# Two long passes, two short ones, and a later norm in the up stage of a transformer block

## The chip, the cores and the metric

The kernel runs on one core of one Trainium2 chip. Its time is device microseconds of one execution. Five engines work side by side, each on a queue of its own in fixed order: TensorE (PE; its loads of the stationary operand are shown apart as PEld), VectorE (DVE), ScalarE (ACT), GpSimd (POOL) and SyncE (SP), which here only issues DMA transfers. They wait for each other by semaphores. TensorE reads SBUF and writes PSUM, which has eight banks of 128 x 512 fp32 numbers.

## The reference, cut to what matters

One block of a model with 256 tokens and width 2048, all in fp32. After three kinds of attention and a gate comes the part that the change touches:

```python
h2 = rms_norm(x, g_ffn)
u = causal_depthwise_conv(h2 @ w_up, conv_w, conv_b)   # w_up: 2048 x 11264, 3 taps along the sequence
u_gate, u_val = split(u, 2)                            # 5632 columns each
x = x + (silu(u_gate) * u_val) @ w_down
```

The causal convolution works on each column of h2 @ w_up by itself: y[t] = w0 u[t-2] + w1 u[t-1] + w2 u[t] + b, with zeros before the first token.

## The kernel before, in words

A fp32 number is split in two parts: hi, rounded to the format that TensorE multiplies at full rate, and lo, what is left. A product of two fp32 matrices is then three products of parts (hi hi, lo hi, hi lo). For a weight tile that is: a DMA to a raw tile (the SP queue), a cast to hi on ScalarE (L141) and a subtraction that gives lo on VectorE (L142), all in `piece`. Raw, hi and lo tiles have four buffers each, so a piece's hi and lo are written when the piece four before it has been read.

**The up stage** (L1133 to L1154) computes the columns of h2 @ w_up transposed, with 128 columns on the partitions and the 256 tokens along the free dimension. It works in 22 *rounds*: for each block of 512 columns (f0) one round for the gate half (s = 0) and one for the value half (s = 1). A round fills four PSUM banks, one for each 128 columns, over 16 k tiles of 128 rows, loaded two at a time: eight pieces, named by their first k tile (k=0, 2, ... 14). The moving operand hT holds hi and lo of the hidden state side by side, 256 columns each. For each k tile and bank there are two passes:

- a *long* pass (L1148): the weight's hi part against all 512 columns of hT. The bank's left half gets hi hi, its right half hi lo.
- a *short* pass (L1149): the weight's lo part against the first 256 columns, added to the left half.

That makes 64 *pairs* a round, 1408 in the stage. They follow each other long, short, long, short.

**The row norm** of h2 isn't applied to hT; it is a factor for each token and may be multiplied in after the product. Its sums are taken from the new x while round one runs. Then L1044 writes the 256 factors to DRAM and L1045 reads them back to all partitions, both on GpSimd's queue, into the tile rbc, 128 x 256.

**The convolution** of one bank is `conv` (L1109 to L1129): a copy of the bank's right half (ScalarE, L1114), the left half added (VectorE, L1116), the product with rbc into a padded tile u (L1117), the three taps (ScalarE L1120, VectorE L1121 and L1122), and for the gate half Silu (L1124), for the value half the product with the gate (L1128) and a split in hi and lo for the next stage (L175, L176). There are two tiles u, used in turn, six tiles y, and two tiles cr for the sum of the halves.

**The order of work.** `later` puts a generator in a list; `tick`, called once a piece (a *step*), lets the two oldest run up to their next `yield`, which may name a number of steps to sit out. So the four convolutions of a round run in the first two steps of the next round, two a step. Beside them two background generators (`weight_sums`, L243 to L274) prepare sums of tiles of w_down for the next stage: loads pre_d on SP, three additions on VectorE (L267 to L269), a store. Within that, a scheduler settles each engine's order, except for instructions given to `in_order`, which stay in the order of the program.

Of the kernel before, what the change touches and what calls it, by code (L numbers as in the profile page):

```python
# [9 lines left out]
F32 = mybir.dt.float32  # L10
F32R = mybir.dt.float32r
AF = mybir.ActivationFunctionType
ALU = mybir.AluOpType
AX = mybir.AxisListType

P = 128
S = 256
# [24 lines left out]
def hybrid_block(  # L42
# [25 lines left out]
    nc = tc.nc  # L68
# [12 lines left out]
    def bank(name):  # L81
        return pp.tile([P, 512], F32, tag="bank", name=name)
# [14 lines left out]
    def later(gen):  # L97
        waiting.append(gen)
# [3 lines left out]
    def tick(beside=True):  # L102
        if beside:
            for g in background:
                next(g, None)
        while waiting and len(active) < WINDOW:
            active.append([waiting.popleft(), 0])
        for a in list(active):
            if a[1] > 0:
                a[1] -= 1  # L110
                continue
            try:
                a[1] = next(a[0]) or 0
            except StopIteration:
                active.remove(a)
# [19 lines left out]
    def piece(src, a, n, name):  # L135
        raw = wp.tile([P, PIECE], F32, tag="raw", name=f"raw_{name}")
        hi = wp.tile([P, PIECE], F32R, tag="hi", bufs=SBUFS, name=f"hi_{name}")
        lo = wp.tile([P, PIECE], F32R, tag="lo", bufs=SBUFS, name=f"lo_{name}")
        m = a * n
        pin(nc.sync.dma_start(raw[:, :m].rearrange("p (a n) -> p a n", a=a), src))  # L140
        pin(nc.scalar.copy(hi[:, :m], raw[:, :m]))  # L141
        pin(nc.vector.tensor_tensor(lo[:, :m], raw[:, :m], hi[:, :m].bitcast(F32), ALU.subtract))  # L142
        return (
            hi[:, :m].rearrange("p (a n) -> p a n", a=a),
            lo[:, :m].rearrange("p (a n) -> p a n", a=a),
        )
# [9 lines left out]
    def product(x_of, w, nk, n0, n, name):  # L156

        ps = [bank(f"{name}_{t}") for t in range(NT)]
        wv = w.rearrange("(k p) n -> p k n", p=P)
        for k in range(0, nk, 2):  # L160
            a = min(2, nk - k)
            wh, wl = piece(wv[:, k : k + a, n0 : n0 + n], a, n, f"{name}_{k}")
            order = [(j, t) for j in range(a) for t in range(NT)]
            if k + a == nk:
                order.sort(key=lambda jt: jt[1])
            for j, t in order:
                xk = x_of(k + j)
                xs_ = xk[:, t * P : (t + 1) * P], xk[:, S + t * P : S + (t + 1) * P]
                three(ps[t][:, :n], *xs_, (wh[:, j], wl[:, j]), k + j == 0, k + j == nk - 1)
            tick()  # L170
        return ps

    def split_to(dst, src):

        nc.scalar.copy(dst[..., :S], src)  # L175
        nc.vector.tensor_tensor(dst[..., S:], src, dst[..., :S].bitcast(F32), ALU.subtract)  # L176
# [25 lines left out]
    def k_tiles(name):  # L202

        most = xt_pool.tile([P, KT - 2, 2 * S], F32R, tag="xt", name=name)
        rest = []

        def at(k):
            if k < KT - 2:
                return most[:, k]
            if not rest:  # L210
                rest.append(xt_pool.tile([P, 2, 2 * S], F32R, tag="xu", name=f"{name}_rest"))
            return rest[0][:, k - KT + 2]

        at.pair = lambda p: most[:, 2 * p : 2 * p + 2]
        return at
# [14 lines left out]
    in_order = tc.keep_in_program_order  # L230
# [343 lines left out]
    def plain_heads(ps, rs, name):  # L574
        y = rows_of(block(f"y_{name}"))
        for t in range(NT):
            nc.scalar.activation(y[:, t], ps[t], AF.Copy, scale=rs[:, t : t + 1])
        return y

    def norm_heads(ps, rs, name):  # L580

        y = plain_heads(ps, rs, name)
        ss = sm.tile([P, NT * 4], F32, tag="hss", name=f"hss_{name}")
        for t in range(NT):
            sq = junk(f"sq_{name}_{t}")
            nc.scalar.activation(sq, y[:, t], AF.Square)
            nc.vector.tensor_reduce(
                ss[:, t * 4 : (t + 1) * 4], sq.rearrange("p (h d) -> p h d", h=4), AX.X, ALU.add
            )
        r = sm.tile([P, NT * 4], F32, tag="hr", name=f"hr_{name}")  # L590
        rsqrt_mean(r, ss, NT * 4, HD, name)
        for t in range(NT):
            yt = y[:, t].rearrange("p (h d) -> p h d", h=4)
            nc.vector.tensor_tensor(
                yt, yt, r[:, t * 4 : (t + 1) * 4].unsqueeze(2).to_broadcast([P, 4, HD]), ALU.mult
            )
        return y
# [74 lines left out]
    for k in range(KT):  # L672
# [18 lines left out]
        for _ in range(0 if k < 3 else 1 if k < 8 else 3):  # L691
            if squares:
                j, t = squares.popleft()
# [9 lines left out]
    y = norm_heads(kv[0], rstd_m, "mk")  # L703
# [26 lines left out]
    ps = proj(C_MQ, MEM_W, "mq")  # L730
# [5 lines left out]
    y = norm_heads(ps, rstd, "mq")  # L736
# [30 lines left out]
    for c in range(3):  # L767
        ps = proj(c * 512, 512, f"f{c}")
        qk[c] = heads_of(block(f"qk_fox{c}"))
        y = norm_heads(ps, rstd, f"f{c}")  # L770
# [5 lines left out]
    ps = proj(1536, 512, "f3")  # L776
# [3 lines left out]
    ps = proj(2048, 262, "f4")  # L780
# [74 lines left out]
    for c in range(3):  # L855
        ps = proj(C_SB + c * 512, 512, f"s{c}")
        qs[c] = heads_of(block(f"qk_sb{c}"))
        y = plain_heads(ps, rstd, f"s{c}")
# [49 lines left out]
    ps = proj(C_SB + 1536, 512, "s3")  # L908
# [4 lines left out]
    ps = proj(C_SB + 2048, 256, "s4")  # L913
# [39 lines left out]
    for m in range(2):  # L953
        gate = []
        for b, plan in enumerate(g_plans[m]):
# [40 lines left out]
            if not plan:  # L996
                biases()
                for n in range(2):
                    ps = proj(c0 + n * 512, 512, f"g{n}_{b}")
# [12 lines left out]
        for n in range(2):  # L1012
            acc = gate[branches[0][3]][n]
            for i, (w, k0, nk, b) in enumerate(branches):
                ps = product(lambda k: oT[:, k0 + k], w[0], nk, (2 * m + n) * 512, 512, f"b{2 * m + n}_{b}")
# [15 lines left out]
    hT = k_tiles("hT")  # L1031
    rbc = cst.tile([P, S], F32, name="rbc")
# [49 lines left out]
    for i in range(2):  # L1082
        background.append(
            weight_sums(
                lambda name, i=i: ff.tile([P, 1024], F32, tag=f"end{i}", bufs=1, name=name), 8, 6, delay=14 + 2 * i
# [3 lines left out]
    def a_pair(p):  # L1089
        if p < FA // 2:  # L1090
            return aT[:, 2 * p : 2 * p + 2]
        if p not in ends:
            ends[p] = ff.tile([P, 2, 2 * S], F32R, tag=f"end{p - FA // 2}", bufs=1, name=f"end_{p}")
        return ends[p]

    uv = ctx.enter_context(ExitStack())
    cp = uv.enter_context(tc.tile_pool(name="cp", bufs=2))
    upv = w_up[0].rearrange("(k p) n -> p k n", p=P)
    pads = []

    def padded():
        for i in range(2):
            u = cp.tile([P, S + 2], F32, bufs=1, name=f"u_{i}")
            nc.vector.memset(u[:, 0:2], 0.0)
            pads.append(u)

    ys = {}

    def conv(ps, f, s):  # L1109
        if not pads:  # L1110
            padded()
        ct = s * FT + f
        cr = cp.tile([P, S], F32, tag="cr", bufs=2, name=f"cr_{f}_{s}")
        nc.scalar.copy(cr, ps[:, S:])  # L1114
        u = pads[f % 2]
        nc.vector.tensor_tensor(cr, cr, ps[:, :S], ALU.add)  # L1116
        nc.vector.tensor_tensor(u[:, 2:], cr, rbc, ALU.mult)  # L1117
        y = cp.tile([P, S], F32, tag="y", bufs=6, name=f"y_{f}_{s}")
        tap = lambda j: taps[:, j, ct : ct + 1]
        nc.scalar.activation(y, u[:, 2:], AF.Identity, scale=tap(2), bias=tap(3))  # L1120
        nc.vector.scalar_tensor_tensor(y, u[:, 1 : S + 1], tap(1), y, ALU.mult, ALU.add)  # L1121
        nc.vector.scalar_tensor_tensor(y, u[:, 0:S], tap(0), y, ALU.mult, ALU.add)  # L1122
        if s == 0:
            nc.scalar.activation(y, y, AF.Silu)  # L1124
            ys[f] = y
        else:
            g = ys.pop(f)
            nc.vector.tensor_tensor(g, g, y, ALU.mult)  # L1128
            split_to(a_pair(f // 2)[:, f % 2], g)  # L1129
        return  # L1130
        yield

    for f0 in range(0, FT, 4):  # L1133
        if f0 == FA:
            assert not halves
            for g in background:
                deque(g, 0)
            background.clear()
        for s in range(2):
            ps = [bank(f"u{f0 + i}_{s}") for i in range(4)]  # L1140
            c0 = s * D_FF + f0 * P
            for k in range(0, KT, 2):
                hi, lo = piece(upv[:, k : k + 2, c0 : c0 + 512], 2, 512, f"u{f0}_{s}_{k}")
                for j in range(2):
                    first, last = k + j == 0, k + j == KT - 1
                    for i in range(4):
                        c = slice(i * P, (i + 1) * P)
                        nc.tensor.matmul(ps[i], lhsT=hi[:, j, c], rhs=hT(k + j), start=first, stop=False)  # L1148
                        nc.tensor.matmul(  # L1149
                            ps[i][:, :S], lhsT=lo[:, j, c], rhs=hT(k + j)[:, :S], start=False, stop=last  # L1150
                        )
                tick()
            for i in range(4):
                later(conv(ps[i], f0 + i, s))  # L1154

# [40 lines left out]
    for nb, plan in enumerate(d_plans):  # L1196
# [5 lines left out]
        for t in range(NT):  # L1202
            for n in range(2):
                c = nb * PIECE + n * 512
                o = xres[:, t, c : c + 512]
                nc.vector.tensor_tensor(o, o, X[t][n], ALU.add)
                if (nb, t, n) == (1, 1, 1):
                    nc.scalar.dma_start(ov[:, t, c : c + 256], o[:, :256])
                    c, o = c + 256, o[:, 256:]
# [35 lines left out]
```

## Time and profile before

| | |
|---|---|
| three runs | 1472.53, 1480.77, 1480.96 us; median 1480.77 |
| the profiled execution | 1473.09 us |
| its span, first to last instruction | 1471.4 us |
| TensorE busy | 1462.6 us, 99% of the span |
| VectorE, ScalarE busy | 81%, 57% |
| up stage | from 746.5 us to 1243 us in the span |
| mean granted clock of TensorE | 0.998 |

How to read it: the page's busy times are for one execution, and a matmul's record lasts longer than the step to the next one, because matmuls overlap; the pace is read from the starts. A line of a group has the source line, the engine, the operation, the output and the inputs, the shape and the count, then busy time in us, the mean of one in ns, and the engine's idle time before them with what ended most of it. A line of the timeline has start and length in us; "x2" means two instructions merged; what stands in brackets is the idle time before it and who ended it. In the list of transfers the last number is us from issue to landing.

### The profile page before, as it was taken

The page shows a single profiled execution, that of the slowest core. Times are in us where ns is not written, and L with a number is a line of the kernel's source. Part 1 is how long each engine was busy: PE and PEld are TensorE (multiplying, and loading weights), DVE is VectorE, ACT ScalarE, POOL GpSimd, SP SyncE. Part 2 cuts the span into 40 slices and gives each one's busy share as a digit, 9 for nine tenths or more (in the row PEclk, how much of TensorE's full clock was granted, in tenths as well). Part 3 has the DMA queues.
Part 4 walks back from the last instruction along what each step waited for, and adds up shares of the span by engine and source line. Part 5 has one row for each costly group of instructions (what it writes and reads, how often), then busy time and mean ns, then how long its engine had stood idle before and what let it go on. Part 6 is the DMA issues. An engine that isn't in the chain of part 4 may idle for free.

```text
span 1471.4 us, 20662 instructions
## 1 busy us (share of the span) xinstructions
PE 1462.6 (99%) x7335; PEld 1236.9 (84%) x7335; DVE 1192.1 (81%) x1816; ACT 838.9 (57%) x1194; POOL 21.7 (1%) x48
## 2 busy tenths in 40 slices
PE   9999999999999999999999999999999999999998
PEld 7888888888888888888887888888888888888887
DVE  5777676777588899997877888888899877997877
ACT  6755454464364455546665556556556565674664
POOL 0000000021000000000000000000000000000000
PEclk9999999999999999999999999999999999999999
DMA  9686787687868576878777998888888866798795
GB/s 310 200 275 192 218 285 215 185 273 217 248 197 277 165 230 201 277 254 274 244 191 239 298 288 283 278 285 286 286 287 285 266 191 200 243 322 273 249 339 218
DMA packets 205606, 369.55 MB, mean 251 GB/s; under 512 B 13578, under 2 KB 82078, under 8 KB 205246
## 3 DMA queue, kind: packets, MB, share of 16 engines
q1 hardware_dynamic: 204094, 365.99, 78.0%
q10 hardware_dynamic: 1328, 2.11, 0.4%
q8 instruction: 57, 0.93, 0.2%
q14 instruction: 47, 0.39, 0.1%
q0 software_dynamic: 80, 0.13, 0.0%
HBM read 335.67 MB, written 32.51 MB: 250 GB/s over the span
## 4 chain that ended last, share of the span: by engine, by line
PE 97%; issue 1%; ACT 1%; DVE 1%; DMA 0%; POOL 0%; POOLq 0%; DVEq 0%
PE u L1148 21%; PE u L1149 11%; PE xd L286 4%; PE xd L288 4%; PE xd L287 4%; PE xg L288 3%; PE xg L287 3%; PE xg L286 3%; PE f L288 2%; PE f L287 2%; PE f L286 2%; PE s L286 2%; PE s L288 2%; PE s L287 2%; PE g L286 2%; PE g L288 2%
## 5 line engine op out<-in xcount | busy, mean ns | idle before, releaser
L1148 PE MATMUL u<-hT,hi_u 128*128 128x512 f32 x1232 | 430.8, 395 | 0.0
L1149 PE MATMUL u<-hT,lo_u 128*128 128x256 f32 x1232 | 342.7, 278 | 3.4 <-DVE lo_u L142 3.4
L1148 PEld LDWEIGHTS u<-hT,hi_u 128*128 128x128 f32 x1232 | 232.3, 189 | 54.0
L142 DVE TENSOR_TENSOR lo_u<-raw_u,hi_u 128x1024 fp32r<-128x1024 f32 x176 | 214.7, 1221 | 61.7 <-ACT hi_u L141 60.7
L141 ACT CAST hi_u<-raw_u 128x1024 fp32r<-128x1024 f32 x176 | 184.6, 1050 | 136.4 <-PE u L1148 120.5
L1149 PEld LDWEIGHTS u<-hT,lo_u 128*128 128x128 f32 x1232 | 232.6, 189 | 3.8 <-DVE lo_u L142 3.8
L281 DVE TENSOR_TENSOR lo_d<-raw_d,hi_d 128x1024 fp32r<-128x1024 f32 x88 | 106.6, 1221 | 20.4 <-ACT hi_d L280 17.6
L280 ACT CAST hi_d<-raw_d 128x1024 fp32r<-128x1024 f32 x88 | 91.9, 1053 | 47.8 <-PE xd L287 22.5
L280 ACT CAST hi_g<-raw_g 128x1024 fp32r<-128x1024 f32 (+1 forms) x64 | 61.7, 972 | 37.9 <-PE xg L287 12.1
L281 DVE TENSOR_TENSOR lo_g<-raw_g,hi_g 128x1024 fp32r<-128x1024 f32 (+1 forms) x64 | 70.8, 1117 | 4.1 <-ACT hi_g L280 4.1
L141 ACT CAST hi_f<-raw_f 128x1024 fp32r<-128x1024 f32 (+1 forms) x40 | 38.6, 967 | 52.1 <-PE f L287 47.3
L142 DVE TENSOR_TENSOR lo_f<-raw_f,hi_f 128x1024 fp32r<-128x1024 f32 (+1 forms) x40 | 44.6, 1118 | 27.9 <-ACT hi_f L141 26.1
L288 PE MATMUL xd<-lo_d,aT 128*128 128x512 f32 x170 | 66.2, 389 | 0.0
L287 PE MATMUL xd<-hi_d,aT 128*128 128x512 f32 x170 | 66.2, 389 | 0.0
L286 PE MATMUL xd<-hi_d,aT 128*128 128x512 f32 x170 | 66.1, 389 | 0.0
L142 DVE TENSOR_TENSOR lo_s<-raw_s,hi_s 128x1024 fp32r<-128x1024 f32 (+1 forms) x40 | 44.7, 1117 | 25.0 <-ACT hi_s L141 24.7
L141 ACT CAST hi_s<-raw_s 128x1024 fp32r<-128x1024 f32 (+1 forms) x40 | 38.4, 961 | 43.9 <-PE s L287 27.0
L1120 ACT ACTIVATE y<-u,taps 128x256 f32<-128x256 f32 x88 | 49.2, 595 | 23.8 <-DVE u L1117 23.8
L1148 PE MATMUL u<-hT_rest,hi_u 128*128 128x512 f32 x176 | 62.1, 394 | 0.0
L142 DVE TENSOR_TENSOR lo_g<-raw_g,hi_g 128x1024 fp32r<-128x1024 f32 x32 | 39.3, 1232 | 22.7 <-ACT hi_g L141 22.4
L141 ACT CAST hi_b<-raw_b 128x1024 fp32r<-128x1024 f32 x32 | 33.5, 1051 | 40.8 <-PE b L287 15.0
L141 ACT CAST hi_g<-raw_g 128x1024 fp32r<-128x1024 f32 x32 | 33.5, 1051 | 37.3 <-PE g L287 35.4
(479 smaller groups left out, 3530.3 us busy)
## 6 DMA issues: line engine op xcount, KB each, us to landing
raw_u<-in_w_up_dram SPq DMA_DIRECT2D x176, 512.0 KB, 5.2
raw_g<-in_w_in_dram SPq DMA_DIRECT2D x96, 512.0 KB, 4.4
raw_d<-in_w_down_dram SPq DMA_DIRECT2D x66, 512.0 KB, 5.3
pre_d<-in_w_down_dram SPq DMA_DIRECT2D x88, 256.0 KB, 4.4
kept_d<-pre_d SPq DMA_DIRECT2D x44, 512.0 KB, 5.5
raw_f<-in_w_in_dram SPq DMA_DIRECT2D x32, 512.0 KB, 4.7
raw_s<-in_w_in_dram SPq DMA_DIRECT2D x32, 512.0 KB, 3.8
raw_o<-in_w_out_dram SPq DMA_DIRECT2D x25, 512.0 KB, 5.4
```

Of the source, the lines that this page charges most:

```text
L141: pin(nc.scalar.copy(hi[:, :m], raw[:, :m]))
L142: pin(nc.vector.tensor_tensor(lo[:, :m], raw[:, :m], hi[:, :m].bitcast(F32), ALU.subtract))
L280: nc.scalar.copy(hi[:, :n], src)
L281: nc.vector.tensor_tensor(lo[:, :n], src, hi[:, :n].bitcast(F32), ALU.subtract)
L286: fix(nc.tensor.matmul(o, lhsT=ah, rhs=w[0], start=first, stop=False))
L287: fix(nc.tensor.matmul(o, lhsT=al, rhs=w[0], start=False, stop=False))
L288: fix(nc.tensor.matmul(o, lhsT=ah, rhs=w[1], start=False, stop=last))
L1120: nc.scalar.activation(y, u[:, 2:], AF.Identity, scale=tap(2), bias=tap(3))
L1148: nc.tensor.matmul(ps[i], lhsT=hi[:, j, c], rhs=hT(k + j), start=first, stop=False)
L1149: nc.tensor.matmul(ps[i][:, :S], lhsT=lo[:, j, c], rhs=hT(k + j)[:, :S], start=False, stop=last)
```

## The change

Two things change, both in the up stage.

The passes of one k tile are done for two banks at a time: two long ones, then their two short ones, then the same for the other two banks. `conv` is cut in two functions: `out_of` empties a bank (copy and add), `taken` does the rest. For rounds after the first they are called one behind the other, as before. For the four banks of the first round there is one generator, `first_convs`: in the first two steps of round two it empties the banks into y tiles; it sits out the third to the sixth; from the seventh on it does the norm, taps and Silu of one convolution a step, so that the last two come in the first two steps of round three. The norm is then given to `in_order`. While this generator lives, it takes one of the two places in `tick`, so in the first steps of round three the value half's convolutions come one a step.

```diff
+    def out_of(ps, dst):
+        nc.scalar.copy(dst, ps[:, S:])
+        nc.vector.tensor_tensor(dst, dst, ps[:, :S], ALU.add)
+        return dst
+
+    def y_tile(f, s):
+        return cp.tile([P, S], F32, tag="y", bufs=6, name=f"y_{f}_{s}")
+
-    def conv(ps, f, s):
-        if not pads:
-            padded()
+    def taken(cr, y, f, s):
         ct = s * FT + f
-        cr = cp.tile([P, S], F32, tag="cr", bufs=2, name=f"cr_{f}_{s}")
-        nc.scalar.copy(cr, ps[:, S:])
         u = pads[f % 2]
-        nc.vector.tensor_tensor(cr, cr, ps[:, :S], ALU.add)
-        nc.vector.tensor_tensor(u[:, 2:], cr, rbc, ALU.mult)
-        y = cp.tile([P, S], F32, tag="y", bufs=6, name=f"y_{f}_{s}")
+        ins = nc.vector.tensor_tensor(u[:, 2:], cr, rbc, ALU.mult)
+        if y is not None:
+            in_order(ins)
+        y = y_tile(f, s) if y is None else y
...
+    def conv(ps, f, s):
+        taken(out_of(ps, cp.tile([P, S], F32, tag="cr", bufs=2, name=f"cr_{f}_{s}")), None, f, s)
         return
         yield
+
+    def first_convs(ps):
+        kept = []
+        padded()
+        for f in range(4):
+            kept.append(out_of(ps[f], y_tile(f, 0)))
+            if f % 2:
+                yield
+        yield 3
+        for f in range(4):
+            taken(kept[f], kept[f], f, 0)
+            yield
...
-                    for i in range(4):
-                        c = slice(i * P, (i + 1) * P)
-                        nc.tensor.matmul(ps[i], lhsT=hi[:, j, c], rhs=hT(k + j), start=first, stop=False)
-                        nc.tensor.matmul(
-                            ps[i][:, :S], lhsT=lo[:, j, c], rhs=hT(k + j)[:, :S], start=False, stop=last
-                        )
+                    for i0 in (0, 2):
+                        two = [(i, slice(i * P, (i + 1) * P)) for i in (i0, i0 + 1)]
+                        for i, c in two:
+                            nc.tensor.matmul(ps[i], lhsT=hi[:, j, c], rhs=hT(k + j), start=first, stop=False)
+                        for i, c in two:
+                            nc.tensor.matmul(
+                                ps[i][:, :S], lhsT=lo[:, j, c], rhs=hT(k + j)[:, :S], start=False, stop=last
+                            )
                 tick()
+            if f0 + s == 0:
+                later(first_convs(ps))
+                continue
```

In the changed kernel the lines are: L1110 and L1111 copy and add, L1120 the norm, L1125 to L1127 the taps, L1129 Silu, L1133 the product with the gate, L1169 the long and L1171 the short pass.

## The prediction

> **What bounds the kernel now.** I read the page's busy line and its chain first, then the costliest groups.
>
> ```profile
> PE 1462.6 (99%) x7335; PEld 1236.9 (84%) x7335; DVE 1192.1 (81%) x1816; ACT 838.9 (57%) x1194; POOL 21.7 (1%) x48
> PE 97%; issue 1%; ACT 1%; DVE 1%; DMA 0%; POOL 0%; POOLq 0%; DVEq 0%
> L1149 PE MATMUL u<-hT,lo_u 128*128 128x256 f32 x1232 | 342.7, 278 | 3.4 <-DVE lo_u L142 3.4
> L1149 PEld LDWEIGHTS u<-hT,lo_u 128*128 128x128 f32 x1232 | 232.6, 189 | 3.8 <-DVE lo_u L142 3.8
> ```
>
> TensorE is the bound almost everywhere: it is 97% of the chain. A change can pay in two ways only: the matmuls follow each other more closely, or TensorE stops less. The group of the short passes shows the only stop of any size: 3.4 us, waiting for a lo tile of VectorE. So two questions: what a pair of passes costs now, and what that stop really costs.
>
> The windows view gives the state of the up stage around the stop and far from it. Columns: busy time of PE, PEld, DVE, ACT and POOL, then granted clock, DMA share, GB/s.
>
> ```profile
> 780.00:785.00 5.00, 2.28 (x7) 1.99 (x8) 4.23 (x10) 3.75 (x6) 0.00 (x0) 0.65 0.34 84
> 900.00:1000.00 100.00, 100.00 (x579) 87.43 (x578) 87.41 (x154) 57.99 (x89) 0.00 (x0) 1.00 0.89 283
> ```
>
> Far from the stop TensorE never idles and VectorE is 87% busy. At the stop TensorE is busy for 2.28 of 5 us and its clock is down to 0.65. The timeline says what happened, on TensorE, VectorE and GpSimd (whose queue issues the two transfers that turn the row norm into rbc):
>
> ```profile
> 764.48 0.86 POOL L1044 DMA_DIRECT2D rstd_row<-scales  x1 [395.59 <-DVE scales L534]
> 773.64 0.57 POOL L1045 DMA_DIRECT2D rbc<-rstd_row  x1 [8.29 <-DMA rstd_row<-scales]
> 770.13 0.77 DVE L1116 TENSOR_TENSOR cr<-cr,u 128x256 f32<-128x256 f32 x2
> 780.77 0.76 DVE L1117 TENSOR_TENSOR u<-cr,rbc 128x256 f32<-128x256 f32 x2 [9.87 <-DMA rbc<-rstd_row]
> 781.45 1.22 DVE L142 TENSOR_TENSOR lo_u<-raw_u,hi_u 128x1024 fp32r<-128x1024 f32 x1
> 778.89 0.39 PE L1148 MATMUL u<-hT,hi_u 128*128 128x512 f32 x1
> 782.72 0.58 PE L1149 MATMUL u<-hT,lo_u 128*128 128x256 f32 x1 [3.44 <-DVE lo_u L142]
> 783.10 0.63 PE L1148 MATMUL u<-hT,hi_u 128*128 128x512 f32 x1
> 788.64 0.40 PE L1148 MATMUL u<-hT,hi_u 128*128 128x512 f32 x1
> ```
>
> VectorE's queue stands for 9.87 us at the norm (L1117) of the first two convolutions, because rbc lands at 780.77. The lo of k=6 is queued behind it and ends at 782.67; TensorE needs it right after 778.89. When the passes go on, each long one takes 0.63 instead of 0.40 until 788.64.
>
> **The price of one pair.** First and last rows of three stretches without idle time, far from the stop:
>
> ```profile
> 1000.00 0.27 PE L1149 MATMUL u<-hT,lo_u 128*128 128x256 f32 x1
> 1003.81 0.28 PE L1149 MATMUL u<-hT,lo_u 128*128 128x256 f32 x1
> 1452.97 0.39 PE L286 MATMUL xd<-hi_d,aT 128*128 128x512 f32 x1
> 1465.66 0.39 PE L288 MATMUL xd<-lo_d,end 128*128 128x512 f32 x1
> 301.00 0.28 PE L288 MATMUL s<-lo_s,xT 128*128 128x256 f32 x1
> 307.48 0.28 PE L288 MATMUL s<-lo_s,xT_rest 128*128 128x256 f32 x1
> ```
>
> Long, short, long, short: 11 pairs in 3.81 us, 346.4 ns a pair. Long behind long: 56 steps in 12.69 us, 226.6 ns. Short behind short: 54 steps in 6.48 us, 120.0 ns. Each has a new stationary operand at each pass.
>
> **Part one, the order of the passes.** All 1408 pairs of the stage (22 rounds of 64) change from L S L S to L L S S. The passes, their loads and their count stay. Of the four steps from one pass to the next, two pairs now have L-S, S-L, L-S, S-L (2 x 346.4 = 692.8 ns); afterwards they have L-L, L-S, S-S, S-L: 226.6 + 120.0 + 346.4 = 693.0. That is 0.1 ns a pair more, 0.14 us over 1408, so I take nothing. The bounds: reading to 0.01 us over 11 pairs is about 1 ns a pair, 1.4 us either way.
>
> What else hangs on the order: the lo tile is needed one long pass (0.23 us) later after the hi tile, the hi tile's last reader comes one short pass earlier, and a round's first bank is complete 0.81 us before the round's end (two long, three short passes) instead of 1.04 (three pairs), which holds up no matmul: the next round writes four other banks.
>
> **Part two, the first four convolutions.** Nothing is added or removed but the place: four copies and four adds (now L1110, L1111) stay where they were, at the first two steps of the second round, and write into the y tiles; the norm (L1120), the taps and Silu come from the seventh step on, one convolution a step. In VectorE's order the norm now stands behind the lo of k=6, 8, 10 and 12 and behind one set of weight sums; in ScalarE's the same hi casts go ahead of the first tap. The order of the SP and GpSimd queues doesn't change, but SP's does run earlier: its loads of raw tiles waited for those lo's.
>
> *What goes.* Between the long passes at 778.89 and 788.64 lie 10 pairs, 3.46 us at the usual pace; they took 9.75. Lost: **6.29 us**, of which 3.6 is the wait beyond the usual step and 2.7 the passes at the low clock.
>
> *What is late next.* Three things could make the lo's late again: their raw tiles, the place of the norm, and the work that piles up behind it. The rows for them:
>
> ```profile
> 767.80 0.39 PE L1148 MATMUL u<-hT_rest,hi_u 128*128 128x512 f32 x1
> 770.22 0.37 SPq L140 DMA_DIRECT2D raw_u<-in_w_up_dram  x1
> raw_u<-in_w_up_dram SPq DMA_DIRECT2D x1, 512.0 KB, 10.4
> 770.63 1.10 SPq L258 DMA_DIRECT2D pre_d<-in_w_down_dram  x1
> pre_d<-in_w_down_dram SPq DMA_DIRECT2D x1, 256.0 KB, 10.7
> 791.12 0.68 DVE L267 TENSOR_TENSOR pre_d<-pre_d 128x512 f32<-128x512 f32 x1
> 792.64 2.35 DVE L142 TENSOR_TENSOR lo_u<-raw_u,hi_u 128x1024 fp32r<-128x1024 f32 x2
> 794.91 0.69 DVE L267 TENSOR_TENSOR pre_d<-pre_d 128x512 f32<-128x512 f32 x1
> 798.71 0.74 DVE L1116 TENSOR_TENSOR cr<-cr,u 128x256 f32<-128x256 f32 x2
> 799.37 0.75 DVE L1117 TENSOR_TENSOR u<-cr,rbc 128x256 f32<-128x256 f32 x2
> 801.36 0.87 DVE L1121 SCALAR_TENSOR_TENSOR y<-u,taps,y 128x256 f32<-128x256 f32 x2
> 802.15 0.88 DVE L1122 SCALAR_TENSOR_TENSOR y<-u,taps,y 128x256 f32<-128x256 f32 x2
> L141 ACT CAST hi_u<-raw_u 128x1024 fp32r<-128x1024 f32 x176 | 184.6, 1050 | 136.4 <-PE u L1148 120.5
> L142 DVE TENSOR_TENSOR lo_u<-raw_u,hi_u 128x1024 fp32r<-128x1024 f32 x176 | 214.7, 1221 | 61.7 <-ACT hi_u L141 60.7
> ```
>
> The k=14 piece of round one starts at 767.80, a piece is 8 pairs or 2.77 us, so round two starts at 770.57 and its k=12 piece at 787.2. The raw tile of k=12 lands at 780.6 (770.22 + 10.4). A cast takes 1.05 and a lo 1.22, so this lo ends at 782.9, 4 us early. The sums behind it need pre_d, landed at 781.3 for the first half and by about 782 for the second, and take 1.5 (791.12 to 792.64): 784.4. There stands the norm, and rbc landed at 780.77. So **it doesn't wait**, with 3.6 us to spare.
>
> Then comes a crowd. From 784.4 up to the lo of k=8 in round three, VectorE's order has five lo's at 1.135 (792.64 to 794.91 for two), one set of sums at 1.5, 17 adds, products and splits at 0.33 (798.71 to 799.37 for two) and 14 taps at 0.395 (801.36 to 802.15 for two): the first four convolutions, and those of the value half, which now run one a step beside them. 5.7 + 1.5 + 5.6 + 5.5 = 18.3, and 1.2 for that lo: 803.9. TensorE needs it at 770.57 + 12 x 2.77 + 0.45 (two long passes) = 804.3. Waits for ScalarE's copies and taps within the chain are not in the sum. I charge **0.5 us**, within 0 (all hidden) and 2 (2.4 of such waits). From there on VectorE has less to do than TensorE (87%).
>
> The granted clock tells what such a rest costs: it fell to 0.65 in the stretch that holds a stop of 3.44 us. By the Trainium skill (TensorE: Matmul & The Clock Gate, Part 1) an idle window of about 3.4 us, free-running, halves the clock; by that rule a stop of 0.5 to 2 us costs itself alone, as I charge it, and if any stop dropped the clock the sum would be about 2.7 us more.
>
> **The sum.** The profiled execution took 1473.09 us, its span 1471.4 and 1.7 around it. 1473.09 - 6.29 + 0.5 = **1467.3**. The three runs shown are 1472.53, 1480.77 and 1480.96: the profile stands at their low end, 7.7 us below the median, and one profile can't say what the other two have more. If that is still there, 1475.0.
>
> **The rivals.**
>
> *rbc comes late.* Before, SP issued nothing from 774.8 to 782.7, as its next load waited for VectorE; now a 512 KB load goes out beside the transfer of rbc. From a landing at 784.4 on, each us is a us more for the lo of k=8. At 786 it is 2.1 in all, 1468.9; at 789, 5.1 and the clock's 2.7, so 1474.6. I take 1471. For it: that transfer and the row before it took 7 to 9 us, and loads beside them over 10. Against: 3.6 us of slack.
>
> *Slower: the second short pass lays its load bare.* A load's record is 189 ns, a short pass's step 120. If the second of two short passes must wait for its whole load, 67 to 69 ns come on each of 704 S-S steps: 48 us, 1515. It decides from 8 ns a step (5.8 us over 704), above which the change loses. Against: the short-behind-short stretch has the same loads at 120.0.
>
> *Faster: short passes pair up well.* Behind a long pass a short one might cost half a long one, 113 ns, and two in a row too: 6.7 ns on 704 steps, 4.7 us, 1462.6. The same stretch speaks against it.
>
> That the norm isn't moved far enough is ruled out as far as the order goes; whether the five steps suffice is the first rival.
>
> **How the numbers follow.** Forecast 0.68, rbc late 0.13, slower 0.09, faster 0.10. The range goes from the faster rival, 1462, to the forecast and the first rival at the level of the median, 1477. About 1% is what a measurement of this kernel can tell from no change; 1467.3 is 0.9% under the median shown and 0.4% under the profile, so most of it is "within 1%". Faster by over 1%: the faster rival and 0.10 of the forecast, 0.20. Slower: 0.09. Within: 0.71.
>
> **What would show it.** The norm's wait for rbc is gone from VectorE's waits, or under 1 us; no short pass waits over 1 us for a lo; the clock stays at 1.00 from 780 to 790; a stretch of the up stage still gives 346 ns a pair, a short pass behind a short one 120. I am wrong if the pair's pace moves by over 4 ns, or if a stop of several us stands near 804.

## The result

| | time, us |
|---|---|
| changed kernel, 9 runs | median 1469.73 (1468.71 to 1470.62) |
| kernel before, 9 runs beside them | median 1480.77 (1472.53 to 1482.69) |
| ratio | 0.9938, 95% interval 0.9919 to 0.9957 |
| changed kernel, the profiled execution | 1469.51, span 1467.8 (before: 1473.09, 1471.4) |

The forecast was 1467.3, within 1462 to 1477, and most likely within 1% of the kernel before. The time fell 0.4 to 0.8%. Two things in it ask for an explanation: the profile lost 3.6 us where the forecast had 5.8, while the median lost 11.

The group of the short passes on the page of the changed kernel:

```profile
L1171 PE MATMUL u<-hT,lo_u 128*128 128x256 f32 x1232 | 242.1, 278 | 0.3 <-DVE lo_u L142 0.3
```

The stop of 3.4 us in front of the short passes has become 0.3. (The group's busy time is less than before because two short passes that overlap are now counted together; it is no gain.) The windows view of the changed kernel, with the columns as in the prediction, shows the place of the old stop and the stretch far from it:

```profile
778.00:790.00 12.00, 12.00 (x71) 10.49 (x70) 9.77 (x14) 7.89 (x10) 0.00 (x0) 1.00 0.98 342
900.00:1000.00 100.00, 100.00 (x575) 87.25 (x575) 87.21 (x154) 59.12 (x95) 0.00 (x0) 1.00 0.89 284
```

TensorE no longer idles there and the clock stays at 1.00. But in the 100 us far from the stop it starts 575 matmuls instead of 579. The timeline of the changed kernel says why, and shows what is left of the wait; "x2" are two passes whose records overlap:

```profile
746.50 0.62 PE L1169 MATMUL u<-hT,hi_u 128*128 128x512 f32 x2
803.97 0.63 PE L1169 MATMUL u<-hT,hi_u 128*128 128x512 f32 x2
804.85 0.50 PE L1171 MATMUL u<-hT,lo_u 128*128 128x256 f32 x2 [0.25 <-DVE lo_u L142]
805.20 0.63 PE L1169 MATMUL u<-hT,hi_u 128*128 128x512 f32 x2
900.40 0.28 PE L1171 MATMUL u<-hT,lo_u 128*128 128x256 f32 x1
1003.51 0.28 PE L1171 MATMUL u<-hT,lo_u 128*128 128x256 f32 x1
1239.22 0.40 PE L286 MATMUL xd<-hi_d,aT 128*128 128x512 f32 x1
```

From 900.40 to 1003.51 lie 148 groups of two long and two short passes: 696.7 ns a group, **348.3 ns a pair**. The same reading of the kernel before:

```profile
746.54 0.39 PE L1148 MATMUL u<-hT,hi_u 128*128 128x512 f32 x1
899.81 0.28 PE L1149 MATMUL u<-hT,lo_u 128*128 128x256 f32 x1
1003.81 0.28 PE L1149 MATMUL u<-hT,lo_u 128*128 128x256 f32 x1
1242.78 0.40 PE L286 MATMUL xd<-hi_d,aT 128*128 128x512 f32 x1
```

300 pairs in 104.00 us: **346.67 ns** (the prediction read 346.4 from 11 pairs). So the up stage, from its first pass to the first one of the next stage, took 496.24 us before and 492.72 after, 3.52 less. The stop that went is 6.29. The pass order gave back 1.67 ns on nearly all of the 1408 pairs, 2.3 us. And the wait at 804 lost 0.53 (1.23 us from one pair of long passes to the next, 803.97 to 805.20, where 0.70 is usual). -6.29 + 2.3 + 0.5 = -3.5: the difference of the two profiles is explained. The difference of the medians isn't; the experiments are about that.

### The profile page after: what moved, and what is told of

Same layout as the page of the kernel before. It is cut to its first block, busy times and chain, and to the rows that moved or that the text cites. A ratio compares the mean times of both kernels' runs of the same rounds, so it can differ in the third digit from the quotient of the medians.

```text
span 1467.8 us, 20662 instructions
## 1 busy us (share of the span) xinstructions
PE 1461.5 (100%) x7335; PEld 1235.3 (84%) x7335; DVE 1191.9 (81%) x1816; ACT 836.6 (57%) x1194; POOL 21.8 (1%) x48
## 4 chain that ended last, share of the span: by engine, by line
PE 97%; DVE 1%; DMA 0%; ACT 0%; SPq 0%; issue 0%; POOL 0%; POOLq 0%; DVEq 0%
PE u L1169 22%; PE u L1171 11%; PE xd L287 4%; PE xd L288 4%; PE xd L286 4%; PE xg L288 3%; PE xg L286 3%; PE xg L287 3%; PE f L288 2%; PE f L286 2%; PE f L287 2%; PE s L286 2%; PE s L288 2%; PE s L287 2%; PE g L286 2%; PE b L288 2%
## 5 line engine op out<-in xcount | busy, mean ns | idle before, releaser
L1169 PE MATMUL u<-hT,hi_u 128*128 128x512 f32 x1232 | 387.0, 395 | 0.0
L1171 PEld LDWEIGHTS u<-hT,lo_u 128*128 128x128 f32 x1232 | 231.3, 188 | 55.3 <-DVE lo_u L142 0.7
L1171 PE MATMUL u<-hT,lo_u 128*128 128x256 f32 x1232 | 242.1, 278 | 0.3 <-DVE lo_u L142 0.3
L1169 PEld LDWEIGHTS u<-hT,hi_u 128*128 128x128 f32 x1232 | 187.6, 189 | 0.1
L1169 PE MATMUL u<-hT_rest,hi_u 128*128 128x512 f32 x176 | 55.3, 395 | 0.0
L286 PE MATMUL xg<-hi_g,xT 128*128 128x512 f32 x140 | 54.5, 389 | 0.0
```

Source lines behind the costliest of these rows:

```text
L286: fix(nc.tensor.matmul(o, lhsT=ah, rhs=w[0], start=first, stop=False))
L1171: nc.tensor.matmul(ps[i][:, :S], lhsT=lo[:, j, c], rhs=hT(k + j)[:, :S], start=False, stop=last)
```

## The experiments

The kernel before ran in every comparison, 74 times in all: 21 times at 1471.29 to 1474.69 (median 1473.3), 53 times at 1479.56 to 1483.61 (median 1481.0), never between. Its profile belongs to the lower group. The 11 runs beside the first four kernels below were all in the upper group; what decides between the groups is not known. The intervals of all ratios are wide because of these two groups, so below I give times, and compare within groups.

### Part two alone, and the order of passes in four forms

The first kernel is the changed one with the passes alternating again, so it has part two alone:

```diff
-                    for i0 in (0, 2):
-                        two = [(i, slice(i * P, (i + 1) * P)) for i in (i0, i0 + 1)]
...
+                    for i in range(4):
+                        c = slice(i * P, (i + 1) * P)
+                        nc.tensor.matmul(ps[i], lhsT=hi[:, j, c], rhs=hT(k + j), start=first, stop=False)
+                        nc.tensor.matmul(
+                            ps[i][:, :S], lhsT=lo[:, j, c], rhs=hT(k + j)[:, :S], start=False, stop=last
+                        )
```

> Only the later norm; the passes go long, short, long, short as before. Theory A (the pass order itself costs 1.6 ns a pair, 348.0 against 346.4): the up stage runs at 346.4 ns a pair and the time is about 2.3 us under the changed kernel's 1469.7, so 1467.4. Rival B (the pace of the changed kernel's stage comes from something in the moved convolutions): 348.0 ns a pair and 1469.7. On the spread: if the before kernel's extra 8 us in two runs of three sit in the stop for rbc, this kernel has none of it, and all runs lie within 2 us.

The second alternates too, but a short pass goes to the bank of the long pass before the last one, so that every step changes the bank (at the end of a piece two short passes stand together, and then two long ones):

```diff
+                        o = (i - 1) % 4
+                        jo = j if i else j - 1
...
+                            ps[o][:, :S], lhsT=lo[:, jo, at(o)], rhs=hT(k + jo)[:, :S], start=False,
```

> Later norm; long and short passes alternate, but a short pass goes to the bank of the long pass before last, so nearly every pass changes bank (15 of 16) as in the changed kernel, while only 2 of 16 neighbours are alike. Theory A1 (neighbours of the same width cost): 346.6 ns a pair, 1467.5 us. Rival A2 (a change of bank at each pass costs 1.6 ns more a pair): 348.0 ns, 1469.7 us.

The third keeps two and two, but takes the two k tiles of a piece for one bank, so that four passes in a row go to the same bank:

```diff
-                for j in range(2):
...
+                for i in range(4):
+                    c = slice(i * P, (i + 1) * P)
+                    for j in range(2):
+                        nc.tensor.matmul(ps[i], lhsT=hi[:, j, c], rhs=hT(k + j), start=k + j == 0, stop=False)
+                    for j in range(2):
+                        nc.tensor.matmul(
+                            ps[i][:, :S], lhsT=lo[:, j, c], rhs=hT(k + j)[:, :S], start=False, stop=k + j == KT - 1
+                        )
```

> Later norm; two long and two short passes as in the changed kernel, but all four into one bank (both k tiles of a piece), so the bank changes once in four passes instead of at each. Theory A1 (neighbours of the same width cost): 348.0 ns a pair, 1469.7 us. Rival A2 (bank changes cost): half a change a pair instead of two, about 345.6 ns a pair, 1466.3 us.

The fourth takes four long passes, then four short ones, for the four banks:

```diff
-                    for i0 in (0, 2):
-                        two = [(i, slice(i * P, (i + 1) * P)) for i in (i0, i0 + 1)]
+                    four = [(i, slice(i * P, (i + 1) * P)) for i in range(4)]
```

> Later norm; four long passes, then four short ones, each into another bank. Theory A1 (neighbours of the same width cost, 1.6 ns a pair for one alike pair of neighbours in two): three in four are alike, 348.8 ns a pair, 1470.8 us. Rival A2 (bank changes): as in the changed kernel, 348.0 ns, 1469.7 us. The step of a short pass behind a short one is to be read here in threes: 120 ns if it is as in the earlier stage.

Measured:

| passes of the up stage | runs | times, us |
|---|---|---|
| alternating (part two alone) | 6 | 1466.77, 1466.99, 1467.72 and 1474.87, 1476.31, 1476.88 |
| alternating, each step another bank | 4 | median 1474.94 (1474.50 to 1475.84) |
| two and two, one bank | 4 | median 1470.11 (1468.80 to 1470.96) |
| four and four | 4 | median 1472.87 (1472.42 to 1473.27) |

The paces, by the first and the last row of long stretches of each timeline. Part two alone (its profile took 1474.87, in the upper group):

```profile
755.02 0.28 PE L1169 MATMUL u<-hT,lo_u 128*128 128x256 f32 x1
802.86 0.28 PE L1169 MATMUL u<-hT,lo_u 128*128 128x256 f32 x1
900.00 0.28 PE L1169 MATMUL u<-hT,lo_u 128*128 128x256 f32 x1
1003.88 0.28 PE L1169 MATMUL u<-hT,lo_u 128*128 128x256 f32 x1
```

138 pairs in 47.84 us, 346.7 ns; then 294 pairs in 103.88, **353.3 ns**. The same instructions in the same order have two paces within one execution, at full clock both times. Alternating with a change of bank at each step (36 groups of 8 pairs, 352.5 ns a pair), two and two in one bank (149 groups of two pairs at 696.7 ns, as in the changed kernel) and four and four (73 groups of 4, 350.8):

```profile
900.35 0.28 PE L1177 MATMUL u<-hT,lo_u 128*128 128x256 f32 x1
1001.87 0.28 PE L1177 MATMUL u<-hT,lo_u 128*128 128x256 f32 x1
```

```profile
899.79 0.28 PE L1169 MATMUL u<-hT,lo_u 128*128 128x256 f32 x1
1003.60 0.28 PE L1169 MATMUL u<-hT,lo_u 128*128 128x256 f32 x1
```

```profile
901.06 0.28 PE L1170 MATMUL u<-hT,lo_u 128*128 128x256 f32 x1
1003.50 0.28 PE L1170 MATMUL u<-hT,lo_u 128*128 128x256 f32 x1
```

What follows. For two and two the bank doesn't matter: the pace is the same in one bank as over two. The alternating kernel with a change of bank at each step took longer than either time put for it, and its mean of 352.5 alone doesn't settle the question, as the double passes at a piece's end also break its order. But inside its pieces, where every step changes the bank as well, both paces of the next paragraphs occur: four pairs from 757.62 to 759.01 take about 347 ns each, three from 952.16 to 953.22 take 353. So nothing speaks for a cost of the change itself. That a long pass next to a long one costs a fixed 1.6 ns falls too: four and four would then have 348.8. And the part-two kernel did not lie within 2 us: three runs came at the 1467.4 of theory A, and three 9 us above it. Its profile flips where a lo tile comes just in time. The weight loads of TensorE and the lo on VectorE in that execution:

```profile
803.21 0.19 PEld L1168 LDWEIGHTS u<-hT,hi_u 128*128 128x128 f32 x1
803.32 0.19 PEld L1169 LDWEIGHTS u<-hT,lo_u 128*128 128x128 f32 x1
803.56 0.19 PEld L1168 LDWEIGHTS u<-hT,hi_u 128*128 128x128 f32 x1
803.75 0.19 PEld L1169 LDWEIGHTS u<-hT,lo_u 128*128 128x128 f32 x1
```

```profile
802.48 1.22 DVE L142 TENSOR_TENSOR lo_u<-raw_u,hi_u 128x1024 fp32r<-128x1024 f32 x1
```

A lo load follows its hi load by 0.11 or 0.12 us; the one at 803.75 follows by 0.19, just behind the lo of k=8 in round three, which ended at 803.70. No matmul waits by the records, and yet from here to the end of the stage a pair takes 353.3; over the 440 us left that is 8.3 us more.

The kernel before has both paces in its profile too. These are its long passes at the start of the stage, ahead of the transposes at 752.19, in which TensorE does other work for 1.6 us:

```profile
747.59 0.40 PE L1148 MATMUL u<-hT,hi_u 128*128 128x512 f32 x1
751.83 0.40 PE L1148 MATMUL u<-hT,hi_u 128*128 128x512 f32 x1
```

12 pairs in 4.24 us are 353.3 ns; behind the transposes it is 346.7. Every profile of a kernel that alternates long and short in one bank shows the same. Nothing is late here, so a late load is not the only thing that can set the pace, and the slow pace can end.

So the theory became: *the alternating order has a quick and a slow pace, and an order change or a late weight load can switch it; two and two has one pace.* From 788.64 the kernel before has 1309 pairs left; 6.67 ns on each are 8.7 us, about the 7.7 between the medians of its two groups.

### Part one alone

> Only the pass order (two long, two short); the first convolutions as before, with their norm in the second step. Theory (the two parts are separate terms: the alternating order runs at 346.6 or at 353.2 ns a pair and may pass from one to the other after a late lo, the two-two order always at 348.3; the stop for rbc costs 6.3 us in either order): 348.3 ns a pair from first to last round, the stop of some 3.5 us with the low clock behind it is there, and all runs lie within 2 us around 1475.5. Rival (the stop itself varies by 8 us between executions): the runs fall in two groups 8 us apart, as before's.

The kernel before with the loop of the passes as in the change, and nothing else:

```diff
-                    for i in range(4):
-                        c = slice(i * P, (i + 1) * P)
+                    for i0 in (0, 2):
+                        two = [(i, slice(i * P, (i + 1) * P)) for i in (i0, i0 + 1)]
```

Ten runs: 1473.01 to 1476.06, median 1474.20, one group, though 3 us wide and not 2. So the rival, a stop that itself varies by 8 us, is out for this order. The stop stands (PE's waits, and a window with PE's busy time, the clock, DMA share, GB/s), and 149 groups of two pairs take 103.81 us, 696.7 ns a group as in the changed kernel:

```profile
PE u L1151 <- DVE lo_u L142: 3.8, 1, 3.8
```

```profile
784.00:789.00 5.00, 5.00 (x21) 0.66 0.40 109
```

```profile
899.73 0.28 PE L1151 MATMUL u<-hT,lo_u 128*128 128x256 f32 x1
1003.54 0.28 PE L1151 MATMUL u<-hT,lo_u 128*128 128x256 f32 x1
```

Against the lower group of before (1473.3) the pass order alone loses 0.9 us; against the upper one (1481.0) it gains 6.8. By the paces it should be 1.67 ns more a pair and 5.0 ns less (2.3 and 6.5 us). Part of the gap to 2.3 is the stop, which in this profile cost 5.6 us and not 6.3.

### No late lo, in both orders

The last wait stands where four convolutions of the value half and the last of the gate half meet. Here the value half's first four are taken one in every two steps:

```diff
+    def second_convs(ps):
+        for f in range(4):
+            yield 1
+            cr = cp.tile([P, S], F32, tag="cr", bufs=2, name=f"cr_{f}_1")
+            taken(out_of(ps[f], cr), None, f, 1)
...
+            if (f0, s) == (0, 1):
+                later(second_convs(ps))
+                continue
```

First with alternating passes (the loop of the first kernel above; "transposes" are the 16 passes at 752 us):

> Later norm, passes alternate as before, and the value half's first four convolutions come one in two steps (steps 2, 4, 6, 8 of round three), so that no lo should be late near 804 us. Theory (the alternating order falls from the quick to the slow pace at a lo that is just in time or late, near 804): no wait of a short pass, 346.6 ns a pair from the transposes at 754 us to the end, all runs within 2 us around 1467.0. Rival (the pace changes at any time, whatever the waits): the runs spread from 1467 to 1476 as with the later norm alone.

Six runs: 1466.77 to 1469.86, median **1467.65**, one group. Both halves of the stage have 300 pairs in 104.00 us, 346.67 ns:

```profile
899.70 0.39 PE L1174 MATMUL u<-hT,hi_u 128*128 128x512 f32 x1
1003.70 0.39 PE L1174 MATMUL u<-hT,hi_u 128*128 128x512 f32 x1
1039.75 0.39 PE L1174 MATMUL u<-hT,hi_u 128*128 128x512 f32 x1
1143.75 0.39 PE L1174 MATMUL u<-hT,hi_u 128*128 128x512 f32 x1
```

This is the fastest kernel of the study, 2.1 us under the changed one (which ran in another comparison). Then the same spread with two and two:

> The changed kernel (two long, two short), and in addition the second convolutions of the value half's first four taken in a step each, as in the version with the alternating order that ran at 1467.65. Theory: the wait of 0.25 us on lo at 804 goes, with what stood around it 0.4 us, and the pace stays 348.3 ns a pair: 1469.3, one group within 1.5 us, against 1466.9 to 1467.7 for the alternating order with the same spread, since 1.67 ns by about 1390 pairs is 2.3 us. Rival: the two orders are worth the same once no lo is late, and the spread alone made the 1467.65: then 1467.0 to 1467.8 here as well.

Ten runs: 1468.57 to 1469.99, median 1469.00, one group, no wait on lo, and 149 groups in 103.81 us:

```profile
899.88 0.28 PE L1177 MATMUL u<-hT,lo_u 128*128 128x256 f32 x1
1003.69 0.28 PE L1177 MATMUL u<-hT,lo_u 128*128 128x256 f32 x1
```

So the rival, that the spread alone made the 1467.65, is out: it is worth 0.7 of the changed kernel's 1469.73, and the quick alternating pace the rest, 1.35 us in the medians where 2.3 were expected. Between the two profiles the up stages, 489.95 and 492.19 us, differ by 2.24; the medians come from different comparisons.

### A lo that is made late

The alternating kernel with the spread again, and additions that nothing uses ahead of one lo on VectorE, far from all else (block f0 = 24, k=8). First eleven:

```diff
+                if (f0, s, k) == (24, 0, 8):
+                    for n in range(11):
+                        in_order(nc.vector.tensor_tensor(junk(f"late_{n}"), xres[:, 0, :512], xres[:, 1, :512], ALU.add))
```

> As the one with no late lo, but eleven additions of 128x512 on VectorE ahead of one lo in the gate round of the seventh block of columns (about 1020 us) make that lo one or two us late. Theory (a late lo can throw the alternating order into its slow pace for the rest of the stage): 346.6 ns a pair before the wait, and behind it either 346.6 or 353.2, in at least some runs 353.2: then 640 pairs at 6.6 ns, 4.2 us more. Times near 1468.5 and near 1472.8. Rival (pace has nothing to do with waits): 346.6 on both sides and 1468.5 in all runs, or a change elsewhere.

> The same late lo and the same spread convolutions, but in the two-two order of the changed kernel. Theory: the wait costs itself alone, 348.3 ns a pair on both sides of it, all runs within 2 us around 1471. Rival (any order has two paces): a change of pace behind the wait here too.

The second is the same with the loop of two and two. Ten runs each. Alternating: six at 1474.01 to 1475.77, four at 1477.22 to 1479.20. Two and two: 1475.44 to 1477.77, one group. TensorE waited longer than I had meant, and the clock fell, to a mean of 0.66 from 1030 to 1040 in both; hence times above the expected ones. The waits of the two kernels:

```profile
PE u L1178 <- DVE lo_u L142: 5.3, 1, 5.3
```

```profile
PE u L1180 <- DVE lo_u L142: 5.2, 1, 5.2
```

Two groups for the alternating order and one for two and two are as expected, but the two lie only 1.45 us apart at their edges (3.7 in the medians, where 4.2 had been put), and the alternating kernel's profile fell in the lower one and shows 346.7 on both sides. So in this kernel the slow pace is inferred from times alone. Then a second look at the kernel before:

> The kernel before, unchanged, to have a second profile of it. Theory: the alternating order of the passes runs at one of two paces, 346.7 or 353.3 ns a pair, and the kernel's two groups of times (about 1473 and about 1481) are these two paces after the stop at 779 to 789. If this execution takes about 1481, its up stage runs at 346.7 before the stop and at 353.3 behind it, about 8.7 us over 1309 pairs, and the stages before the up stage and behind it are as long as in the first profile; if it takes about 1473, 346.7 on both sides and nothing new is learnt. Rival: the groups differ in another place (the first loads, the down stage, the end); then an execution at 1481 shows 346.7 ns a pair throughout.

It took 1472.97, again the lower group: its stop was 4.4 us, its pace behind it 346.7. No profile of the kernel before in its upper group was had. Last, four additions instead of eleven, and three:

```diff
-                    for n in range(11):
+                    for n in range(4):
```

> The alternating order with the spread convolutions and four additions of 128x512 (instead of eleven) ahead of the lo of k=8 of the fourth block of the value half. These additions are work that nothing uses. Four at 0.61 us put this lo about 0.5 to 1 us behind the passes that need it. Theory: a short lateness lets the alternating order flip from 346.7 to 353.3 ns a pair in some executions, without a loss of clock: one group at about 1468.5 (0.7 us of wait), another about 3.9 us above it (6.67 ns by the 590 pairs that are left of the up stage), and in a profile of the upper group 353.3 from this point on. Rival: the pace isn't decided by a late weight load; then one group at 1468.0 to 1469.0.

```diff
-                    for n in range(11):
+                    for n in range(3):
```

> The same with three additions: lo comes between 0.5 us before the passes need it and 0.2 us behind. Theory: at the edge, where the load of the first lo weights comes at all late, the pace flips in some or all executions (1471.5), and in the others stays 346.7 (1467.5); where it is not late at all, 1467.5 throughout. Rival: as with four additions, one group, 1467.4 to 1468.2.

Four: five runs at 1468.05 to 1470.10, five at 1471.64 to 1474.50. Three: 1467.24, 1467.60, 1469.54, and seven at 1471.61 to 1473.47. Both profiles (1471.64 and 1472.22) lie in the upper groups, and both show the flip. With three additions, PE's timeline:

```profile
899.78 0.39 PE L1177 MATMUL u<-hT,hi_u 128*128 128x512 f32 x1
1003.78 0.39 PE L1177 MATMUL u<-hT,hi_u 128*128 128x512 f32 x1
1026.66 1.08 PE L1177 MATMUL u<-hT,hi_u 128*128 128x512 f32 x4
1027.90 0.74 PE L1178 MATMUL u<-hT,lo_u 128*128 128x256 f32 x4 [0.16 <-DVE lo_u L142]
1028.48 0.40 PE L1177 MATMUL u<-hT,hi_u 128*128 128x512 f32 x1
1039.80 0.40 PE L1177 MATMUL u<-hT,hi_u 128*128 128x512 f32 x1
1143.67 0.40 PE L1177 MATMUL u<-hT,hi_u 128*128 128x512 f32 x1
1241.89 0.40 PE L286 MATMUL xd<-hi_d,aT 128*128 128x512 f32 x1
```

300 pairs in 104.00 us ahead of the wait, 294 in 103.87 behind it: 346.67 and **353.3**. From 1028.48 to 1241.89 are 604 pairs at 353.3, 4.0 us more than at the quick pace; the wait itself cost 0.4. With four additions:

```profile
899.68 0.39 PE L1177 MATMUL u<-hT,hi_u 128*128 128x512 f32 x1
1003.68 0.39 PE L1177 MATMUL u<-hT,hi_u 128*128 128x512 f32 x1
1029.69 0.40 PE L1177 MATMUL u<-hT,hi_u 128*128 128x512 f32 x1
1141.70 0.40 PE L1177 MATMUL u<-hT,hi_u 128*128 128x512 f32 x1
```

346.67 and, 317 pairs in 112.01, 353.3. So the flip to the slow pace is shown in three kernels, each time within one execution, and each time it lasts to the end of the stage. Two limits: in the three alternating kernels with additions the scheduler also put one k tile's passes as four long, four short (the x4 rows), so a late load and a broken order aren't told apart there; part two alone has no such break and flipped at a late load. And neither always flips it: by their times two or three of ten runs with three additions stayed quick (the third, 1469.54, lies between), and the profile with eleven did too.

## Why the prediction was right, and where not

- **The stop goes: right.** No rest of it is left, the clock holds 1.00, and part two alone, in its quick runs, takes 1466.8 to 1467.7 against 1473.09 - 6.29 = 1466.8.
- **The norm doesn't wait for rbc: right.** It was put at 784.4 with rbc at 780.77. GpSimd's and VectorE's timelines of the changed kernel:

```profile
773.58 0.57 POOL L1045 DMA_DIRECT2D rbc<-rstd_row  x1 [8.46 <-DMA rstd_row<-scales]
```

```profile
784.90 0.43 DVE L269 TENSOR_TENSOR pre_d<-pre_d 128x256 f32<-128x256 f32 x1
785.24 0.42 DVE L1120 TENSOR_TENSOR u<-y,rbc 128x256 f32<-128x256 f32 x1
803.58 1.22 DVE L142 TENSOR_TENSOR lo_u<-raw_u,hi_u 128x1024 fp32r<-128x1024 f32 x1
```

  The transfer of rbc took 7.1 us, so it landed at 780.7; the norm ran at 785.24 without idle time ahead of it. The rival with a late rbc is out.
- **The crowd ahead of the lo of k=8 in round three: right in kind, its size by luck.** The sum put the end of that lo at 803.9, in time for TensorE at 804.3; it came at 804.80. The chain of work was right: from the norm to the start of that lo it took 18.34 us, where 18.3 had been put, without a wait in it. The 0.9 us came in ahead of it: ScalarE's cast for k=12 waited for its raw tile until 781.49, where 780.6 had been put, and so the norm ran at 785.24 and not at 784.4. The cost is 0.53 here, and 0.7 in the medians of the kernels with and without it. The 0.5 had been charged for waits within the chain, and there are none; that as much came from another cause is luck.
- **A short stop costs itself alone: right.** The 1.09 us wait with four additions left the clock at 1.00. Behind the stops of 3.4 us (the kernel before), 3.8 (part one alone) and 5.2 and 5.3 (eleven additions) the granted clock was 0.50 for some us; the means of 0.65 and 0.66 above hold full clock too. In the kernel before (columns as in the prediction):

```profile
783.00:788.00 5.00, 5.00 (x16) 4.25 (x17) 4.96 (x12) 4.97 (x8) 0.00 (x0) 0.50 0.44 110
```

  The Trainium skill (TensorE: Matmul & The Clock Gate, Part 1) puts half the clock behind an idle window of about 3.4 us, and these stops agree with it; where between 1.1 and 3.4 the bound lies, no run here shows.
- **The pass order costs nothing: wrong**, and this is the step that failed. The sum of steps, 226.6 + 120.0 + 346.4 = 693.0, took steps of uniform streams for those of a mixed one. Measured are 696.67. By the starts between 900 and 1000 us of the changed kernel, a long pass behind a long one takes 232.9 on average and not 226.6, a short one behind a short one 114.6 and not 120.0, and the other two together 349.2 and not 346.4. So the step of 120 for a short pass behind a short one, which the prediction named as a sign of being right, is not there either. For four and four 1403.3 are measured, where the same sum gives 1386.2. Each order has a pace of its own, which must be measured. It cost 2.3 us where 1.4 had been put as the bound; with 2.3 in its place the forecast would have been 1469.6, and the median is 1469.73. What was named as the sign of an error, a pace that moves by over 4 ns, didn't come: it moved by 1.67 against the profile.
- **The level of the median runs: left open there, found here.** The 7.7 us that the median had over the profile are most likely the slow pace of the alternating order behind the stop. That this order has the slow pace is shown in the first 5 us of the kernel before and, for hundreds of us, in other kernels; that it had it behind the stop in the upper runs of the kernel before is not shown. It follows only from the size (8.7 against 7.7 us) and from the groups going away with two and two, whose five kernels each ran in one group. If it is so, the changed kernel gains so much against the median because its order doesn't fall into that pace: the part that was taken as nothing costs 2.3 us against the quick runs and is worth 6.5 against the slow ones. The forecast started from the quick level without knowing of the two; that the median came within 2.4 us of it is in part luck.
- **The slower rival (a bare load) and the faster one (short passes pairing well): both out.** With a bare load a pair would take 381 ns (half of 67 to 69 ns more), with the short passes paired well 343; it takes 348.3. The faster rival had one step right: a short pass behind a short one does take 114.6, near its 113. The dearer long steps take more than that back.

## What to carry to other kernels

A pace of mixed matmul widths can't be summed from the steps of uniform streams; read it from a stretch of the very order, over hundreds of starts, and ask whether another execution has another. When a kernel's times fall in two groups, look for one stretch in which the same instructions have two paces: a profile from one group can't show it, but a version that is pushed over on purpose can. A change may then be worth more by the state that it avoids than by the wait that it removes.

## What the runs showed of the hardware

- A stream of 512 and 256 columns in turn, each with its own stationary operand, has two stable paces, 346.67 and 353.33 ns a pair, at full clock. In the quick one the steps from one long pass to the next repeat every two pairs (343 and 350 ns), in the slow one every three (349, 350 and 361). In one profile the change from quick to slow coincided with a load that came 0.08 us late and lasted for the 440 us that were left; in every profile of the kernels that alternate long and short in one bank the pace was slow ahead of 16 other passes and quick behind them.
- The fitted periods of all orders, as means, are whole multiples of 3.33 ns: 104 and 106 for a pair, 209 for two and two, 421 for four and four, 846 for eight pairs with a change of bank.
- In two and two, four passes in a row into one bank cost no more than passes that change the bank (696.7 ns a group in both). Why each order has its pace, and why the alternating one has two, stays open.
